# A hybrid decoder step on one core: where the norms' inverse roots are taken, and how they are spread over the partitions

## The chip, the core and the metric

One NeuronCore of a Trainium2 chip runs the whole program. The metric is the time of one execution in microseconds (us) of device time. Five engines matter: TensorE (PE, with its weight loads as PEld), VectorE (DVE), ScalarE (ACT), GpSimd (POOL), and SyncE (SP), which issues the DMAs. Each engine works through its own queue in order, and a semaphore holds an instruction until what it needs has been written.

## The reference, cut to what matters

Two layers run over 512 prompt tokens and 64 sample tokens (8 sequences of 8). Layer 0 mixes tokens by pooling, layer 1 by a gated delta rule ("GDN"). Each layer has two residual branches, and each branch has a norm before it and one after it.

```python
def rms_norm(x, gain):
    xf = x.astype(jnp.float32)
    y = xf * lax.rsqrt(jnp.mean(xf * xf, axis=-1, keepdims=True) + EPS)
    return (y * gain.astype(jnp.float32)).astype(x.dtype)

def l2norm(x):
    xf = x.astype(jnp.float32)
    return xf * lax.rsqrt(jnp.sum(xf * xf, axis=-1, keepdims=True) + EPS)
...
    for i in range(DEPTH):
        h = rms_norm(x, norm_mix_pre[i])
        ...
        x = x + rms_norm(m, norm_mix_post[i])
        h = rms_norm(x, norm_ffn_pre[i])
        x = x + rms_norm(swiglu(h, ffn_w_in[i], ffn_w_out[i]), norm_ffn_post[i])
```

`m` is the mixer's output of `h`. Inside the GDN mixer, q and k of each head go through `l2norm`, and the output of each head through `rms_norm` before it is gated.

## The kernel before, in words

Activations lie transposed: 1024 channels as 8 chunks of 128 partitions, the 576 tokens along the free dimension. The tokens are worked in two parts (`hf.i` 0 and 1), cut at a different token in different stages: 240 and 336 in the pooling mixer, 288 and 288 in the feed-forward of layer 0, 256 and 320 in layer 1. Every large matmul is done in three products of rounded halves (`mm3`: high by high, high by low, low by high), with weights split on the fly: ACT rounds them to `wh`, DVE or POOL subtracts to get `wl`.

The stages follow each other: the pooling mixer of layer 0 with its norms, the feed-forward of layer 0, then GDN (four groups of heads; `project` makes q, k, v of a group, `core` runs the delta rule, `zgate` norms and gates the output), its output product, norms, and the feed-forward of layer 1.

**Norms between the stages.** `add_sq` (ACT squares, DVE or POOL adds) leaves per partition the sum of squares of each token in `nacc`. `rstd` then does four things:

- PE multiplies each block of 128 tokens of `nacc` with a column of ones: `ps_n<-ones,nacc`, so that the sums of a block stand one per partition in one PSUM column.
- The inverse root `nrc` of these two or three columns is taken. With `on_dve` false this is ACT's `Sqrt` and DVE's `reciprocal`. With `on_dve` true it is `rsqrt` on DVE alone: `nv` (mean plus epsilon), a first guess from the bits of the number, and three Newton steps of three instructions each through `nt`.
- PE spreads `nrc` over all partitions: a matmul of the column, broadcast to 128x128, with the identity, one per block (`ps_n<-ident,nrc`).
- `post_norm` or `pre_norm` multiply the 8 chunks with gain and root on DVE.

`rstd` is called twelve times: four times in layer 0 after the mixer, four times in `finish0` after the feed-forward of layer 0, four times in layer 1 after GDN's output product. `on_dve` is true for the second part of the tokens in `post_pre` only, that is in four of the twelve. The norm at the very end (`finish1`) has its own code and stays as it is.

**Roots inside GDN.** For each of the four groups, `project` takes the inverse root of 20 columns (`rn` from `rv`) by `rsqrt` on DVE, and `gate_norm` that of 20 columns of `oss` by ACT's `Sqrt` and DVE's `reciprocal`.

**What sets the order.** No instruction is issued where it is written: the class `Plan` records all of them with what they depend on, prices each by formulas in `cost`, and orders them by a list scheduler whose priorities are shifted by numbers in the two tables of `CHOSEN`. An operation written as `EITHER` goes to DVE or POOL, whichever the planner finds better. Where PE would otherwise be idle for long, the planner puts in matmuls whose result nobody uses (`ps_w<-ones`). All recorded operations carry one line number in the profile, that of the planner's call, so groups are told apart by the names of tiles.

Of the kernel before, what the change touches and what calls it, by code (L numbers as in the profile page):

```python
# [11 lines left out]
F32 = mybir.dt.float32  # L12
F32R = mybir.dt.float32r
I32 = mybir.dt.int32
AF = mybir.ActivationFunctionType
ALU = mybir.AluOpType
# [37 lines left out]
MAGIC = float(0x5F3759DF)  # L54
# [6 lines left out]
class Plan:  # L61
# [576 lines left out]
    def cost(self, eng, method, out, ins, k):  # L638
# [26 lines left out]
        if eng == "POOL":  # L665
# [4 lines left out]
            elif method == "affine_select":  # L670
                t = 1.1 * n + 190
            else:
                bc = any(list(x.ap)[-1][0] == 0 for x in ins if self.size(x) > 1)
                t = (1.75 if bc else 2.2) * n + 180
# [1854 lines left out]
```

## Time and profile before

| | us |
|---|---|
| median of three runs | 1506.8 (1504.59 to 1508.99) |
| the profiled execution, its time | 1506.02 |
| the profiled execution, its span | 1504.3 |
| ACT busy in it | 838.9 (56%) |
| POOL busy in it | 111.1 (7%) |

The granted TensorE clock has a mean of 0.998 over the span. An engine's busy time is the union of its instructions' spans. A matmul's span overlaps the next one's, so a PE that is "busy" all the time can still be one that waits a little before each instruction; the pace of PE is better read from the starts of successive rows of the timeline. An fp32 matmul leaves two records, a transpose and an fp32r matmul one.

### The profile page before, as it was taken

To read this page: it belongs to the slowest core of one execution; us is meant where nothing else is said; L and a number is where in the kernel's file an instruction comes from. 1 tells how busy PE (TensorE), PEld (TensorE's weight loads), DVE (VectorE), ACT (ScalarE), POOL (GpSimd) and SP (SyncE) were. 2 spreads that over 40 slices of the span, in tenths; PEclk is the share of its full clock that TensorE was granted. 3 is DMA by queue.
4 is the path that set the end of the run, shared out by engine and by line. 5 is a ranking of instruction groups with operands and counts; after the bars stand their busy time and mean duration, and the time that the engine had idled before them with its cause. 6 is when DMAs were issued, how large, how long until landed. Compare 5 with 4: busy or idle time off the path is not lost.

```text
span 1504.3 us, 30115 instructions
## 1 busy us (share of the span) xinstructions
PE 1482.4 (99%) x11748; PEld 1438.1 (96%) x11748; DVE 1131.3 (75%) x2291; ACT 838.9 (56%) x1826; POOL 111.1 (7%) x240
## 2 busy tenths in 40 slices
PE   8999999999999999999999999999999999999997
PEld 8999999999999899899899899999999999999997
DVE  7995566778678697897898889557797576766855
ACT  7754443435455886675784784545574543533654
POOL 4200000000002100010121120000110000000000
PEclk9999999999999999999999999999999999999999
DMA  7642323233456433344334434757653332323262
GB/s 199 180 140 84 104 78 102 72 112 91 137 145 165 116 94 95 106 129 133 100 114 127 130 114 124 213 162 205 211 178 111 94 91 87 93 81 112 75 175 88
DMA packets 322821, 186.96 MB, mean 124 GB/s; under 512 B 13163, under 2 KB 315596, under 8 KB 322671
## 3 DMA queue, kind: packets, MB, share of 16 engines
q1 hardware_dynamic: 322679, 185.04, 42.8%
q8 instruction: 92, 1.51, 0.4%
q14 instruction: 50, 0.41, 0.1%
HBM read 154.72 MB, written 30.52 MB: 123 GB/s over the span
## 4 chain that ended last, share of the span: by engine, by line
PE 83%; DVE 6%; issue 4%; ACT 4%; DMA 2%; POOL 1%; SPq 0%; DVEq 0%; POOLq 0%; ACTq 0%
PE ps_A L804 26%; PE ps_B L804 26%; PE ps_m L804 18%; PE ps_s L804 4%; PE ps_k L804 4%; PE ps_x L804 2%; DVE wl L804 2%; PE ps_e L804 1%; DVE ac L804 1%; ACT wh L804 1%; PE ps_g L804 1%; PE ps_n L804 1%; ACT Uw L804 0%; PE ps_w L800 0%; DVE Uw L804 0%
## 5 line engine op out<-in xcount | busy, mean ns | idle before, releaser
L804 ACT ACTIVATE wh<-wraw 128x1024 fp32r<-128x1024 f32 (+4 forms) x214 | 207.9, 973 | 159.6 <-PE ps_A L804 77.0
L804 DVE TENSOR_TENSOR wl<-wraw,wh 128x1024 fp32r<-128x1024 f32 (+4 forms) x214 | 240.3, 1124 | 59.8 <-ACT wh L804 49.4
L804 PE MATMUL ps_m<-hH,wh 128*128 128x320 f32 (+1 forms) x832 | 248.5, 311 | 0.4 <-ACT u L804 0.3
L804 PE MATMUL ps_m<-hL,wh 128*128 128x320 f32 (+1 forms) x832 | 248.1, 309 | 0.0
L804 PE MATMUL ps_m<-hH,wl 128*128 128x320 f32 (+1 forms) x832 | 245.2, 308 | 0.0
L804 PEld LDWEIGHTS ps_m<-hH,wh 128*128 128x128 f32 x832 | 154.5, 189 | 4.7 <-issue 1.3
L804 PEld LDWEIGHTS ps_m<-hH,wl 128*128 128x128 f32 x832 | 154.0, 189 | 3.8 <-issue 2.1
L804 PEld LDWEIGHTS ps_m<-hL,wh 128*128 128x128 f32 x832 | 154.7, 189 | 1.6 <-issue 0.3
L804 PE MATMUL ps_B<-hL,wh 128*128 128x288 f32 (+2 forms) x420 | 123.6, 304 | 0.2 <-POOL hL L804 0.2
L804 PE MATMUL ps_B<-hH,wl 128*128 128x288 f32 (+2 forms) x420 | 123.1, 304 | 0.0
L804 PE MATMUL ps_B<-hH,wh 128*128 128x288 f32 (+2 forms) x420 | 122.3, 304 | 0.4 <-ACT hH L804 0.4
L804 PE MATMUL ps_A<-aH,wh 128*128 128x288 f32 (+2 forms) x408 | 115.4, 297 | 0.0
L804 PE MATMUL ps_A<-aH,wl 128*128 128x288 f32 (+2 forms) x408 | 115.1, 297 | 0.0
L804 PE MATMUL ps_A<-aL,wh 128*128 128x288 f32 (+2 forms) x408 | 115.1, 296 | 0.0
L804 PE MATMUL ps_A<-hH,wh 128*128 128x288 f32 (+2 forms) x396 | 108.8, 290 | 0.3 <-ACT nsq L804 0.2
L804 PE MATMUL ps_A<-hL,wh 128*128 128x288 f32 (+2 forms) x396 | 108.8, 288 | 0.0
L804 PE MATMUL ps_A<-hH,wl 128*128 128x288 f32 (+2 forms) x396 | 107.9, 289 | 0.2 <-DVE wl L804 0.2
L804 DVE SCALAR_TENSOR_TENSOR ac<-u,cwt,ac 128x600 f32<-128x600 f32 x96 | 79.8, 845 | 2.9 <-ACT ac L804 2.4
L804 PE MATMUL ps_B<-aH,wh 128*128 128x288 f32 x296 | 82.0, 296 | 0.0
L804 PE MATMUL ps_B<-aL,wh 128*128 128x288 f32 x296 | 81.7, 295 | 0.0
L804 PE MATMUL ps_B<-aH,wl 128*128 128x288 f32 x296 | 81.4, 295 | 0.3 <-DVE wl L804 0.3
L804 PEld LDWEIGHTS ps_B<-hL,wh 128*128 128x128 f32 x420 | 77.9, 188 | 0.6 <-POOL hL L804 0.5
(457 smaller groups left out, 4019.5 us busy)
## 6 DMA issues: line engine op xcount, KB each, us to landing
wraw<-in_ffn_w_in_dram SPq DMA_DIRECT2D x64, 512.0 KB
wraw<-in_gdn_w_in_dram SPq DMA_DIRECT2D x53, 512.0 KB
graw<-in_ffn_w_in_dram SPq DMA_DIRECT2D x36, 512.0 KB
wraw<-in_ffn_w_out_dram SPq DMA_DIRECT2D x26, 448.0 KB
wraw<-in_gdn_w_out_dram SPq DMA_DIRECT2D x21, 512.0 KB
wraw<-in_ffn_w_out_dram SPq DMA_DIRECT2D x32, 320.0 KB
St<-in_state_gdn_rec_dram SPq DMA_DIRECT2D x32, 256.0 KB
out_dram<-St SPq DMA_DIRECT2D x32, 256.0 KB
```

The lines of the kernel that those rows point to most:

```text
L804: calls[e](*a, **k)
```

## The change

All inverse roots in the twelve calls of `rstd`, in `project` and in `gate_norm` are now taken by one GpSimd instruction: a `tensor_tensor` with the operation power, whose second operand is a column of -0.5, broadcast. [...] The spreading over the partitions is a PE transpose of the broadcast column, block by block, in place of a matmul with the identity. Blocks that overlap are transposed whole.

```diff
+    half = cst.tile([P, 1], F32, name="half")
+    POOL.memset(half, -0.5)
...
-    def rsqrt(y, v, t):
-
-        DVE.tensor_scalar(y.bitcast(I32), v.bitcast(I32), -0.5, MAGIC, op0=mult, op1=add)
-        for _ in range(3):
-            DVE.scalar_tensor_tensor(out=t, in0=y, scalar=-0.5, in1=v, op0=mult, op1=mult)
-            DVE.tensor_tensor(t, t, y, op=mult)
-            DVE.scalar_tensor_tensor(out=y, in0=t, scalar=1.5, in1=y, op0=add, op1=mult)
+    def rsqrt(y, v):
+
+        POOL.tensor_tensor(y, v, half.to_broadcast([P, y.shape[1]]) if len(y.shape) == 2 else
+                           half.unsqueeze(2).to_broadcast([P, y.shape[1], y.shape[2]]), op=ALU.pow)
...
-        if on_dve:
-
-            v, t = (halftile(tp, w, hf, 1, (P, 4))[:, :nb] for w in ("nv", "nt"))
-            DVE.tensor_scalar(v, ps[:, :nb], 1.0 / D, EPS, op0=mult, op1=add)
-            rsqrt(rc, v, t)
-        else:
-            ACT.activation(rc, ps[:, :nb], AF.Sqrt, bias=eps_c, scale=1.0 / D)
-            DVE.reciprocal(rc, rc)
+        DVE.tensor_scalar(rc, ps[:, :nb], 1.0 / D, EPS, op0=mult, op1=add)
+        rsqrt(rc, rc)
         pr = bank("n%d" % hf.i)[:, :hf.n]
-        for i in range(nb):
-            e = min((i + 1) * P, hf.n)
-            PE.matmul(pr[:, i * P:e], rc[:, i:i + 1].to_broadcast([P, P]), ident[:, i * P - offs[i]:e - offs[i]],
-                      start=True, stop=True)
+        for i, o in enumerate(offs):
+            PE.transpose(pr[:, o:o + P], rc[:, i:i + 1].to_broadcast([P, P]), ident)
...
-                        vt_ = pp.tile([P, 2, SP1, 4], F32, name="rv", tag="rv", bufs=1)
-                        DVE.tensor_scalar(vt_[:, 0, :SPANS], ksq, EPS, None, op0=add)
-                        DVE.tensor_scalar(vt_[:, 0, SPANS], pst, EPS, None, op0=add)
-                        rsqrt(rn, vt_[:, 0], vt_[:, 1])
+                        vt_ = pp.tile([P, SP1, 4], F32, name="rv", tag="rv", bufs=1)
+                        DVE.tensor_scalar(vt_[:, :SPANS], ksq, EPS, None, op0=add)
+                        DVE.tensor_scalar(vt_[:, SPANS], pst, EPS, None, op0=add)
+                        rsqrt(rn, vt_)
...
-            ACT.activation(oss, oss, AF.Sqrt, bias=eps_c, scale=1.0 / P)
-            DVE.reciprocal(oss, oss)
+            DVE.tensor_scalar(oss, oss, 1.0 / P, EPS, op0=mult, op1=add)
+            rsqrt(oss, oss)
```

The planner gets a price for the power operation, and the two tables `CHOSEN` hold other numbers throughout, so the order of the whole program is another one. In the table only this changes in kind (first line of each):

```diff
-                t = (1.75 if bc else 2.2) * n + 180
+                t = 9.0 * n + 400 if k.get("op") == ALU.pow else (1.75 if bc else 2.2) * n + 180
...
-        "0: 5989 57171 74663 91275 358 77336 9426 78983 26827 86304 93802 31029 25971 93959 57698 79197 68511 "
```

Counted over the whole program, ACT's table loads go from 26 to 18, ACT's `Sqrt` instructions on `nrc` and `oss` from 15 to 3, and the 32 matmuls `ps_n<-ident,nrc` become 32 transposes. The matmuls that only fill idle time (`ps_w`) go from 42 to 44.

**PE, at the last of the twelve roots** (layer 1, second part of the tokens; `ps_A` is the feed-forward of the first part, which needs nothing of this root, `ps_B` that of the second part, which needs all of it). Before:

```order
L804 MATMUL ps_A<-hH,wh 128x256
L804 MATMUL ps_n_2913<-ident,nrc 128x128 x2
L804 MATMUL ps_n_2913<-ident,nrc 128x64
L804 MATMUL ps_A<-hL,wh 128x256
L804 MATMUL ps_A<-hH,wl 128x256 x2
L800 MATMUL ps_w<-ones 128x128 x2
L804 MATMUL ps_B<-hH,wh 128x320 x3
```

After, the same place:

```order
L747 MATMUL ps_A<-hL,wh 128x256
L747 MATMUL ps_A<-hH,wl 128x256 x2
L747 MATMUL ps_A<-hH,wh 128x256
L747 MATMUL ps_n_2907<-ident,nrc 128x128 x3
L747 MATMUL ps_A<-hL,wh 128x256
L747 MATMUL ps_A<-hH,wl 128x256
L747 MATMUL ps_A<-hH,wh 128x256
```

Three `ps_A` matmuls and two fillers stood between the spreading of the root and the first `ps_B`; now thirteen `ps_A` matmuls stand there, and no filler.

**DVE, at the same root.** `nv`, `nt` and `nrc` are the columns of the root, `yo<-x,prm,ps_n` multiplies the chunks with it. Before:

```order
L804 TENSOR_SCALAR nv<-ps_n_2908 128x3
L804 TENSOR_TENSOR nsq<-nsq,ps_A 128x256
L804 TENSOR_SCALAR nrc<-nv 128x3
L804 TENSOR_TENSOR aL<-nsq,aH 128x256
L804 SCALAR_TENSOR_TENSOR nt<-nrc,nv 128x3
L804 TENSOR_TENSOR wl<-wraw,wh 128x1024
L804 TENSOR_TENSOR nt<-nt,nrc 128x3
L804 TENSOR_TENSOR aL<-nsq,aH 128x256
L804 SCALAR_TENSOR_TENSOR nrc<-nt,nrc 128x3
```

After:

```order
L747 TENSOR_TENSOR wl<-wraw,wh 128x1024
L747 TENSOR_SCALAR nrc<-ps_n_2904 128x3
L747 TENSOR_TENSOR nsq<-nsq,ps_A 128x256
L747 TENSOR_TENSOR aL<-nsq,aH 128x256 x2
L747 SCALAR_TENSOR_TENSOR yo<-x_2781,prm,ps_n_2907 128x320 x4
```

Behind the rows of before come six more Newton instructions and then `yo<-x`; in the change the power stands on POOL's queue, and `yo<-x` is the fourth instruction behind the `tensor_scalar`.

**DVE, at the root of q and k in the first group of GDN** (`rv` holds the sums, `rn` the roots, `nk` and `rq` are made from them). Before:

```order
L804 TENSOR_SCALAR rv<-ps_x 128x4
L804 TENSOR_SCALAR rn<-rv 128x20
L804 SCALAR_TENSOR_TENSOR rv<-rn,rv 128x20
L804 TENSOR_TENSOR rv<-rv,rn 128x20
L804 SCALAR_TENSOR_TENSOR rn<-rv,rn 128x20
```

After:

```order
L747 TENSOR_SCALAR rv<-ksq 128x16
L747 COPY u<-cstt 128x8x3
L747 TENSOR_SCALAR rv<-ps_x 128x4
L747 TENSOR_TENSOR nk<-rn,rv 128x5x2
L747 TENSOR_SCALAR rq<-rn 128x5x2
```

Before, ten instructions on `rn` and `rv` stood between the `rv<-ps_x` row and `nk`; now `nk` follows at once and waits for POOL.

More of the change, by code (lines that the diff above doesn't have):

```diff
@@ L53 @@
 EPS = 1e-6
-MAGIC = float(0x5F3759DF)
 UW = CW - 1 + SEQ
@@ L1279, in add_sq, with rstd @@
             EITHER.tensor_tensor(acc[0], acc[0], sq, op=add)
-    def rsqrt(y, v, t):
-        DVE.tensor_scalar(y.bitcast(I32), v.bitcast(I32), -0.5, MAGIC, op0=mult, op1=add)
-        for _ in range(3):
-            DVE.scalar_tensor_tensor(out=t, in0=y, scalar=-0.5, in1=v, op0=mult, op1=mult)
-            DVE.tensor_tensor(t, t, y, op=mult)
-            DVE.scalar_tensor_tensor(out=y, in0=t, scalar=1.5, in1=y, op0=add, op1=mult)
-    def rstd(tp, acc, hf, on_dve=False):
+    def rsqrt(y, v):
+        POOL.tensor_tensor(y, v, half.to_broadcast([P, y.shape[1]]) if len(y.shape) == 2 else
+                           half.unsqueeze(2).to_broadcast([P, y.shape[1], y.shape[2]]), op=ALU.pow)
+    def rstd(tp, acc, hf):
         offs = [min(o, hf.n - P) for o in range(0, hf.n, P)]
@@ L1296, in rstd, with post_norm @@
         rc = halftile(tp, "nrc", hf, 1, (P, 4))[:, :nb]
-        if on_dve:
-            v, t = (halftile(tp, w, hf, 1, (P, 4))[:, :nb] for w in ("nv", "nt"))
-            DVE.tensor_scalar(v, ps[:, :nb], 1.0 / D, EPS, op0=mult, op1=add)
-            rsqrt(rc, v, t)
-        else:
-            ACT.activation(rc, ps[:, :nb], AF.Sqrt, bias=eps_c, scale=1.0 / D)
-            DVE.reciprocal(rc, rc)
+        DVE.tensor_scalar(rc, ps[:, :nb], 1.0 / D, EPS, op0=mult, op1=add)
+        rsqrt(rc, rc)
         pr = bank("n%d" % hf.i)[:, :hf.n]
-        for i in range(nb):
-            e = min((i + 1) * P, hf.n)
-            PE.matmul(pr[:, i * P:e], rc[:, i:i + 1].to_broadcast([P, P]), ident[:, i * P - offs[i]:e - offs[i]],
-                      start=True, stop=True)
-        return pr
-    def post_norm(tp, x, m, acc, hf, gpost, acc2, on_dve=False):
-        r = rstd(tp, acc, hf, on_dve)
+        for i, o in enumerate(offs):
+            PE.transpose(pr[:, o:o + P], rc[:, i:i + 1].to_broadcast([P, P]), ident)
+        return pr
+    def post_norm(tp, x, m, acc, hf, gpost, acc2):
+        r = rstd(tp, acc, hf)
         for c in range(NC):
@@ L1322, in post_norm, with pre_norm @@
                 add_sq(tp, acc2, xc, c, hf)
-    def pre_norm(tp, x, acc, hf, gpre, on_dve=False, keep=None):
-        r = rstd(tp, acc, hf, on_dve)
+    def pre_norm(tp, x, acc, hf, gpre, keep=None):
+        r = rstd(tp, acc, hf)
         at = slice(hf.o, hf.o + hf.n)
@@ L1335, in post_pre @@
         acc2 = []
-        post_norm(tp, x, m, acc, hf, gpost, acc2, hf.i == 1)
-        pre_norm(tp, x, acc2, hf, gpre, hf.i == 1, keep=m)
+        post_norm(tp, x, m, acc, hf, gpost, acc2)
+        pre_norm(tp, x, acc2, hf, gpre, keep=m)
     class Strassen:
@@ L1873, in finish @@
                         rn = pp.tile([P, SP1, 4], F32, name="rn", tag="rn", bufs=1)
-                        vt_ = pp.tile([P, 2, SP1, 4], F32, name="rv", tag="rv", bufs=1)
-                        DVE.tensor_scalar(vt_[:, 0, :SPANS], ksq, EPS, None, op0=add)
-                        DVE.tensor_scalar(vt_[:, 0, SPANS], pst, EPS, None, op0=add)
-                        rsqrt(rn, vt_[:, 0], vt_[:, 1])
-                        DVE.tensor_tensor(nk[:, :, hh], rn[:, :, 0:2], vt_[:, 0, :, 0:2], op=mult)
+                        vt_ = pp.tile([P, SP1, 4], F32, name="rv", tag="rv", bufs=1)
+                        DVE.tensor_scalar(vt_[:, :SPANS], ksq, EPS, None, op0=add)
+                        DVE.tensor_scalar(vt_[:, SPANS], pst, EPS, None, op0=add)
+                        rsqrt(rn, vt_)
+                        DVE.tensor_tensor(nk[:, :, hh], rn[:, :, 0:2], vt_[:, :, 0:2], op=mult)
                         DVE.tensor_scalar(rq[:, :, hh], rn[:, :, 2:4], float(P) ** -0.5, None, op0=mult)
```

879 rows, old and new, of the table CHOSEN are left out of this document.

## The prediction

> **What bounds the kernel now.** I read the page first: the busy times, then the chain that ended last, then the windows by stage.
>
> ```profile
> PE 1482.4 (99%) x11748; PEld 1438.1 (96%) x11748; DVE 1131.3 (75%) x2291; ACT 838.9 (56%) x1826; POOL 111.1 (7%) x240
> ...
> PE 83%; DVE 6%; issue 4%; ACT 4%; DMA 2%; POOL 1%; SPq 0%; DVEq 0%; POOLq 0%; ACTq 0%
> ```
>
> PE has work almost all the time, and it holds 83% of the chain. So time is won where PE gets less to do, or where PE waits; an instruction less on ACT or DVE counts only where PE waits for it. The windows by stage (length, then busy us and count by engine) tell where that can be.
>
> ```profile
> 0.00:80.00 80.00, 75.03 (x579) 70.94 (x580) 67.62 (x184) 57.99 (x136) 25.97 (x83) 1.00 0.71 196
> 420.00:480.00 60.00, 58.83 (x454) 57.15 (x453) 51.40 (x107) 31.34 (x60) 8.52 (x12) 1.00 0.60 166
> 560.00:720.00 160.00, 157.69 (x1486) 147.22 (x1485) 132.83 (x346) 99.25 (x278) 14.04 (x31) 1.00 0.42 118
> 720.00:880.00 160.00, 157.29 (x1337) 146.09 (x1336) 142.07 (x355) 110.25 (x354) 28.53 (x57) 1.00 0.43 119
> 1062.00:1120.00 58.00, 57.31 (x431) 56.05 (x430) 53.46 (x124) 36.59 (x70) 12.47 (x14) 1.00 0.59 180
> 1120.00:1440.00 320.00, 320.00 (x2403) 319.57 (x2402) 222.28 (x332) 148.21 (x225) 0.00 (x0) 1.00 0.33 96
> ```
>
> The feed-forward (1120 to 1440 us) is PE alone, without a gap, and has no root in it. The twelve roots between the stages lie in 0:80, 420:480 and 1062:1120, where DVE is busy 85%, 86% and 92%; those of GDN lie where DVE is busy 83% and 89%. PE's visible idle time there is small: 5.0, 1.2, 2.3, 2.7 and 0.7 us.
>
> **Term 1, PE's work.** 32 fp32 matmuls become 32 transposes. The tile's rows and PE's timeline at the last root give the price of both.
>
> ```profile
> L804 PE MATMUL ps_n<-ident,nrc x64: 195/275/376, 29.6 to 1111.7; 128*128 128x128 f32 x44, 128*128 128x32 f32 x8, 128*128 128x112 f32 x4, 128*128 128x80 f32 x4
> ...
> 1101.30 0.27 PE L804 MATMUL ps_n<-ident,x 128*128 128x128 f32 x1
> 1101.33 0.37 PE L804 MATMUL ps_A<-hL,wh 128*128 128x256 f32 x1
> ...
> 1111.07 0.28 PE L804 MATMUL ps_A<-hH,wh 128*128 128x256 f32 x1
> 1111.19 0.78 PE L804 MATMUL ps_n<-ident,nrc 128*128 128x128 f32 x6
> 1111.77 0.36 PE L804 MATMUL ps_A<-hL,wh 128*128 128x256 f32 x1
> 1112.22 0.60 PE L800 MATMUL ps_w<-ones 128*128 128x128 f32 x4
> 1113.18 0.71 PE L804 MATMUL ps_B<-hH,wh 128*128 128x320 f32 x3 [0.36 <-ACT hH L804]
> 1116.14 0.60 PE L804 MATMUL ps_n<-ident,x 128*128 128x128 f32 x4
> 1116.49 0.39 PE L804 MATMUL ps_B<-hH,wl 128*128 128x320 f32 x1
> ```
>
> 64 records for 32 matmuls: two each. Three of them hold PE from 1111.19 to 1111.77, 0.58 us or 0.193 each; four transposes from 1116.14 to 1116.49, 0.35 us or 0.088 each. Saved: 32 x 0.105 = **3.4 us**. It is nothing if a transpose of a broadcast column left two records; it is 5.2 us if a transpose costs only 0.03, as the one at 1101.30 does, which stands alone between two `ps_A`. I take 3.4, since most of the new ones stand in threes and twos. Nothing has to hide it: PE is full on both sides.
>
> [...]
>
> **Term 2, the Newton chain ahead of PE.** On DVE's, ACT's and PE's timelines the last root goes:
>
> ```profile
> 1107.18 0.16 DVE L804 TENSOR_SCALAR nv<-ps_n 128x3 f32<-128x3 f32 x1
> ...
> 1110.77 0.16 DVE L804 SCALAR_TENSOR_TENSOR nrc<-nt,nrc 128x3 f32<-128x3 f32 x1
> 1112.08 3.75 DVE L804 SCALAR_TENSOR_TENSOR yo<-x,prm,ps_n 128x320 f32<-128x320 f32 x8 [1.15 <-PE ps_n L804]
> ...
> 1112.66 3.68 ACT L804 ACTIVATE hH<-yo 128x320 fp32r<-128x320 f32 x8
> ```
>
> From 1107.18 to 1110.93 the root takes 3.75 us, since `wl` and `aL` work is mixed in. PE then runs out: fillers (`ps_w`) from 1112.22, and the first `ps_B` at 1113.18 on the first `hH`. That is 0.96 us of PE. In the change the root is one `tensor_scalar` (0.16) and one power, and thirteen `ps_A` matmuls (13 x 0.12 = 1.6 us, by the row at 1111.07 and the start of the next) stand behind the spreading, against the 1.0 us that `yo` and `hH` need. The wait goes: **-1.0 us**. The same chain at the second root of part 1 in layer 0 leaves fewer waits to win, since the 5.0 us of idle time in 0:80 are mostly the start; I take **-0.5 us**. The other two Newton roots stand where PE has feed-forward work: nothing. What is late next is DVE itself, at 92%: ends 0 and -2.5 us for the term.
>
> **The power's own price.** No row shows it. The nearest on POOL:
>
> ```profile
> L804 POOL MEMSET oss<- x4: 102/104/106, 483.6 to 803.5; 128x4 f32 x4
> ...
> L804 POOL TENSOR_SCALAR_AFFINE_SELECT par<-ones 32x1 f32<-32x1 f32 x4 | 2.0, 493 | 0.2
> ...
> L804 POOL TENSOR_TENSOR vt<-vt,oss x4: 1049/1268/1587, 652.1 to 896.5; 128x512 f32<-128x512 f32 x4
> ```
>
> A few columns written cost 0.1 us, one column computed 0.49, 512 columns of a broadcast product 1.27. I take 0.5 us, the row nearest in size, with ends 0.1 and 1.3. On top come held ports, as POOL's and DVE's timelines show:
>
> ```profile
> 457.07 1.68 POOL L804 TENSOR_TENSOR hL<-nh,hH 128x288 fp32r<-128x288 f32 x1 [19.77 <-ACT hH L804]
> 456.51 1.20 DVE L804 TENSOR_TENSOR wl<-wraw,wh 128x1024 fp32r<-128x1024 f32 x1
> 459.85 0.81 POOL L804 TENSOR_TENSOR hL<-nh,hH 128x288 fp32r<-128x288 f32 x1 [0.33 <-ACT hH L804]
> 71.89 1.81 POOL L804 TENSOR_SCALAR_AFFINE_SELECT eyo<-eyo 128x512 f32<-128x512 f32 x1
> 72.92 0.76 DVE L804 SCALAR_TENSOR_TENSOR nt<-nrc,nv 128x3 f32<-128x3 f32 x1
> ```
>
> POOL's `hL` took 1.68 us beside a DVE subtraction, twice the 0.81 that the next one takes at 459.85; a DVE step of 0.16 took 0.76 beside POOL. So a power can come up to a `wl` (1.2 us) late, and can hold DVE.
>
> **Term 3, the eight roots that ACT took.** At the first root of `finish0`:
>
> ```profile
> 449.45 0.24 ACT L804 ACTIVATE nrc<-ps_n,epsd 128x3 f32<-128x3 f32 x1
> 449.73 0.18 DVE L804 RECIPROCAL nrc<-nrc 128x3 f32<-128x3 f32 x1 [0.58 <-ACT nrc L804]
> 449.96 0.85 PE L804 MATMUL ps_n<-ident,nrc 128*128 128x128 f32 x6 [0.32 <-DVE nrc L804]
> ```
>
> Root and reciprocal take 0.46 us; `tensor_scalar` and power 0.16 + 0.05 + 0.5, some 0.25 more. PE waited 0.32 us here already. Two of the eight stand so that PE feels it, the first of 0:80 and this one: **+0.4 us** (ends -0.3 and +4, see the slow rival).
>
> **Term 4, GDN.**
>
> ```profile
> L804 DVE SCALAR_TENSOR_TENSOR rv<-rn,rv x12: 171/178/182, 522.4 to 876.8; 128x20 f32<-128x20 f32 x12
> L804 DVE TENSOR_SCALAR rn<-rv x4: 173/176/177, 522.2 to 874.2; 128x20 int32<-128x20 int32 x4
> ...
> L804 DVE RECIPROCAL oss<-oss x4: 266/271/276, 651.7 to 1023.2; 128x20 f32<-128x20 f32 x4
> ...
> L804 ACT ACT_TABLE_LOAD x25 | 32.1, 1283 | 1.2 <-issue 0.8
> ```
>
> Per group DVE loses ten instructions of 0.178, 1.8 us, and gets a wait of some 0.7 us in `nk`, with the subtractions of weights queued behind it; `oss` is 0.1 cheaper. That is 4 x 1.2 = 4.8 us of DVE's queue. ACT loses eight table loads of 1.283 and twelve roots of about 0.25: 13.3 us of 838.9. PE visibly idles 5.0 us in 560:880, beside DVE at 86%, so about a quarter of DVE's gain should reach it: **-1.5 us** with ACT's share (ends 0 and -5).
>
> **Sum.** -3.4 - 1.5 + 0.4 - 1.5 = **-6.0 us** against the profiled execution (span 1504.3, its time 1506.02, 0.8 under the median): **1500.0 us**. The whole order is new as well; two fillers more are 0.4 us of PE at most, and where they stand PE has nothing else to do. I give the order no sign and 3 us to both sides.
>
> **Rivals.**
> - *Only PE's work goes.* PE is busy 157.3 to 157.7 of 160 us in GDN, so ACT's and DVE's savings may be hidden throughout; then -3.4 and a little: 1503. Against it stands the filler wait at 1112.22.
> - *The power is late, and the kernel slower.* The place is the eight roots that were ACT's, four of them at a stage's first part with PE dry behind them. With the high price (1.3), a `wl` ahead on the port (1.2) and `tensor_scalar`, a root takes 2.7 us against 0.46: four times +2.2, while the Newton roots gain nothing: -3.4 + 9 = +5.6, 1512. It decides where power and hold together pass 0.46 - 0.2 + 3.4/4 = 1.1 us; over 0.3% slower needs some 2.5. POOL's 7% load speaks against it; DVE at 85% to 92%, full of `wl`, for it.
> - *The first power is special.* If POOL has to fetch code before it, the first root (29.6 us) comes late by that time L, and PE, with 5 us idle in that window already, shows L in full: 1500 + L. It eats the whole gain at L = 6. No row here shows an L. [...]
> - *DVE is the real bound of GDN.* Then all of its 4.8 us and a part of ACT's come through: -3.4 - 2.5 - 5 = 1495.
>
> **Chances.** Forecast (1497 to 1502) 0.46; only PE's work 0.25; slow power 0.11; first power 0.06; DVE bound 0.12. A measurement of this kernel tells about 0.3% from no change, that is under 1502.3 or over 1511.3 us. Faster: 0.46 + 0.12 = 0.58; same 0.25 + 0.06 = 0.31; slower 0.11. The range takes in the DVE bound with 3 us of order below, and the first power with 3 us above: 1492 to 1509.
>
> **What would show it.** Term 1: `ps_n<-ident,nrc` with 32 records in place of 64, three to 0.27 us. Term 2: no filler at the last root, and `yo<-x` some 1.5 us behind its `tensor_scalar`. The power: POOL rows `nrc<-nrc,half` near 0.5 us; over 1 us, or a first one far longer, speaks for a rival. Term 4: DVE near 1117 us busy, 18 table loads, and PE idling less than 5.0 us in 560:880. It is wrong if PE's idle time grows in 0:80 or 420:480.

## The result: 1.7% slower, and the profile after

| | before | after |
|---|---|---|
| median, us | 1506.8 (5 runs) | 1531.69 (1529.0 to 1533.96, 5 runs) |
| ratio, with its 95% interval | | 1.0166 (1.015 to 1.0182) |
| profiled execution, its time and its span, us | 1506.02, 1504.3 | 1529.0, 1527.3 |

The change costs 25 us. Where they came from is read from the starts of the first matmuls of each stage in the two timelines: `ps_e` opens GDN (with the mixer's projections), `ps_A` with a start over 1000 us opens layer 1's norms and feed-forward, `ta` the bulk of that feed-forward.

| stage, us | before | after | difference |
|---|---|---|---|
| up to the first `ps_e` | 452.0 | 448.8 | -3.2 |
| GDN, to the first `ps_A` of layer 1 | 582.7 | 610.6 | +27.9 |
| norms of layer 1, to the first `ta` | 103.7 | 101.0 | -2.7 |
| the rest | 365.9 | 366.8 | +0.9 |

So both places outside GDN got shorter, and GDN alone lost it all. The page of the changed kernel, busy times and chain:

```profile
PE 1484.5 (97%) x11720; PEld 1439.4 (94%) x11720; DVE 1123.7 (74%) x2209; ACT 831.6 (54%) x1806; POOL 147.2 (10%) x263
...
PE 55%; DVE 5%; issue 3%; POOL 2%; DMA 2%; ACT 1%; SPq 0%; DVEq 0%; POOLq 0%; ACTq 0%
```

PE's busy time did not fall by 3.4 us but grew by 2. (The shares of the chain add up to 68% here, so its 55% can't be set beside the 83% of before.) The windows of the changed kernel (length, then busy us of PE, PEld, DVE, ACT, POOL with counts; behind them the granted clock) show two things at once:

```profile
480.00:560.00 80.00, 76.41 (x570) 70.40 (x569) 58.47 (x149) 57.70 (x150) 13.56 (x25) 0.96 0.35 94
560.00:720.00 160.00, 152.63 (x1450) 143.48 (x1449) 126.22 (x311) 99.08 (x276) 24.79 (x45) 0.98 0.40 112
720.00:880.00 160.00, 153.29 (x1290) 142.32 (x1288) 132.54 (x313) 105.62 (x327) 23.33 (x46) 0.98 0.40 114
880.00:1040.00 160.00, 153.44 (x1289) 144.82 (x1288) 112.17 (x262) 87.90 (x239) 19.74 (x26) 0.99 0.49 143
```

PE idles 3.6, 7.4, 6.7 and 6.6 us there, 24.2 in all; before it was 0.3, 2.3, 2.7 and 0.6, 6.0 in all. Over the whole of GDN, which now ends at 1059.4 us, it is 27.3 us against 6.5. And the clock, 1.00 in all four windows before, is below it: PE is "busy" for longer because it runs slowly for a while. POOL's groups name the cause (mean ns behind the busy time, then the idle time ahead):

```profile
L747 POOL TENSOR_TENSOR rn<-rv,half 128x20 f32<-128x20 f32 x4 | 14.1, 3529 | 13.5 <-DVE rv L747 13.5
L747 POOL TENSOR_TENSOR oss<-oss,half 128x20 f32<-128x20 f32 x4 | 14.1, 3526 | 85.0 <-DVE oss L747 85.0
L747 POOL TENSOR_TENSOR nrc<-nrc,half 128x3 f32<-128x3 f32 x8 | 9.0, 1122 | 405.0 <-DVE nrc L747 405.0
L747 POOL TENSOR_TENSOR nrc<-nrc,half 128x2 f32<-128x2 f32 x4 | 5.0, 1251 | 70.8 <-DVE nrc L747 70.8
```

A power of 20 columns takes 3.53 us, of 2 or 3 columns a mean of 1.25 and 1.12. The planner had it at 9 ns per column and 400, that is 0.58 us for 20 columns, so its order holds little behind which the other 3 us could hide. What happens then, at the first `rn` (DVE's and PE's timelines of the changed kernel, in brackets the wait and its releaser):

```profile
517.57 0.16 DVE L747 TENSOR_SCALAR rv<-ps_x 128x4 f32<-128x4 f32 x1 [0.73 <-PE ps_x L747]
521.38 0.59 DVE L747 TENSOR_TENSOR nk<-rn,rv 128x10 f32<-128x10 f32 x1 [3.65 <-POOL rn L747]
...
521.55 0.31 PE L747 MATMUL ps_m<-hH,wh 128*128 128x320 f32 x1
525.45 1.19 PE L747 MATMUL ps_k<-qk 128*128 128x256 f32 x2 [3.59 <-DVE QD L747]
526.08 0.83 PE L747 MATMUL ps_m<-hL,wh 128*128 128x320 f32 x1
```

Nothing on DVE's queue passes the waiting `nk`: DVE stands 3.65 us there, with the steps to `QD` queued behind it, and PE stands 3.6 us for `QD`. The row at 521.55 is the last of PE's work that was planned in parallel. At the first `oss` (rows of POOL, ACT, DVE and PE) a third queue joins in:

```profile
638.85 3.53 POOL L747 TENSOR_TENSOR oss<-oss,half 128x20 f32<-128x20 f32 x1 [1.10 <-DVE oss L747]
642.34 4.28 POOL L747 TENSOR_SCALAR_AFFINE_SELECT QD<-QD 128x512 f32<-128x512 f32 x4
643.01 4.92 ACT L747 ACTIVATE QD<-QD,ngs 128x128 f32<-128x128 f32 x16 [3.19 <-POOL QD L747]
642.42 2.14 DVE L747 TENSOR_TENSOR vt<-vt,oss 128x512 f32<-128x512 f32 x2 [2.72 <-POOL oss L747]
649.50 2.04 PE L747 MATMUL ps_k<-qk 128*128 128x256 f32 x4 [6.48 <-DVE QD L747]
```

The masks `QD` stand behind the power on POOL itself, ACT waits for them, DVE waits for `oss`, and PE is dry for 6.5 us. Then comes the second price, in three windows of the changed kernel around the wait at 521.9:

```profile
516.60:523.40 6.80, 5.26 (x37) 4.79 (x35) 2.31 (x9) 6.71 (x19) 5.80 (x6) 1.00 0.44 122
523.40:530.20 6.80, 4.75 (x17) 4.26 (x17) 5.25 (x17) 0.90 (x5) 0.00 (x0) 0.50 0.29 80
530.20:533.60 3.40, 3.40 (x22) 3.19 (x22) 2.93 (x8) 3.38 (x11) 0.00 (x0) 1.00 0.00 0
```

While PE waits, its clock is halved, and stays so for 6.8 us, well into the work that follows. In the trace this happens five times in GDN: at 523.4 and 646.3 us for 6.8 us each, at 772.6, 803.3 and 895.5 us for 3.4 us each, 23.8 us at half speed. PE has work in 17.9 of them (4.75, 3.50, 3.40, 3.40 and 2.84 us), so this is worth up to 9 us.

### The profile page after: what moved, and what is told of

It reads as the page before. It is cut to its first block, busy times and chain, and to the rows that moved or that the text cites. A ratio compares the mean times of both kernels' runs of the same rounds, so it can differ in the third digit from the quotient of the medians.

```text
span 1527.3 us, 29975 instructions
## 1 busy us (share of the span) xinstructions
PE 1484.5 (97%) x11720; PEld 1439.4 (94%) x11720; DVE 1123.7 (74%) x2209; ACT 831.6 (54%) x1806; POOL 147.2 (10%) x263
## 4 chain that ended last, share of the span: by engine, by line
PE 55%; DVE 5%; issue 3%; POOL 2%; DMA 2%; ACT 1%; SPq 0%; DVEq 0%; POOLq 0%; ACTq 0%
PE ps_m L747 17%; PE ps_A L747 14%; PE ps_B L747 13%; PE ps_s L747 5%; PE ps_k L747 4%; PE ps_x L747 2%; DVE wl L747 1%; POOL oss L747 1%; POOL rn L747 1%; DVE vt L747 1%; DVE ac L747 1%; DVE yo L747 0%; DMA vt<-z_d 0%; DMA yo<-y_d 0%; DVE nacc L747 0%
## 5 line engine op out<-in xcount | busy, mean ns | idle before, releaser
L747 DVE TENSOR_TENSOR wl<-wraw,wh 128x1024 fp32r<-128x1024 f32 (+4 forms) x213 | 237.8, 1117 | 61.0 <-ACT wh L747 40.4
L747 PE MATMUL ps_m<-hH,wh 128*128 128x256 f32 (+1 forms) x832 | 249.7, 315 | 0.1
L747 PE MATMUL ps_B<-aL,wh 128*128 128x288 f32 x296 | 86.0, 296 | 0.0
L747 PE MATMUL ps_B<-aH,wh 128*128 128x288 f32 x296 | 85.1, 296 | 0.0
L747 PE MATMUL ps_B<-aH,wl 128*128 128x288 f32 x296 | 84.5, 296 | 0.2 <-DVE wl L747 0.2
L747 PEld LDWEIGHTS ps_B<-hH,wh 128*128 128x128 f32 x420 | 77.8, 188 | 0.1
```

The source lines that it names most:

```text
L747: calls[e](*a, **k)
```

## The experiments

Two theories at first. **Wide powers**: the eight powers of 20 columns are longer than their cover. **Order**: the new order is worse in itself, and the powers only happen to stand there. In the table, the ratio is to the kernel before, timed beside each run.

| run | median, us | ratio (95%) |
|---|---|---|
| wide_mult | 1498.84 | 0.9947 (0.9929 to 0.9965) |
| all_mult | 1496.62 | 0.9935 (0.9917 to 0.9952) |
| before_wide_pow | 1515.82 | 1.0058 (1.0036 to 1.008) |
| spread_only | 1506.39 | 0.9997 (0.9986 to 1.0009) |
| spread_and_narrow_pow | 1508.99 | 1.0013 (1.0001 to 1.0024) |
| wide_in_pieces | 1523.25 | 1.0111 (1.0091 to 1.0131) |
| before_plain | 1552.96 | 1.0308 (1.029 to 1.0326) |
| after_plain | 1570.1 | 1.0432 (1.0414 to 1.0451) |
| priced_plain | 1549.43 | 1.0292 (1.0277 to 1.0308) |
| norms_plain | 1559.03 | 1.035 (1.0332 to 1.0369) |
| priced | 1566.07 | 1.0394 (1.0367 to 1.0421) |
| before_searched | 1517.47 | 1.0072 (1.005 to 1.0094) |
| priced_searched | 1515.54 | 1.0058 (1.0041 to 1.0076) |
| norms_searched | 1515.41 | 1.0058 (1.0036 to 1.0081) |

### The same order without the wide powers

The planner still plans a power; only where it is issued does another operation stand, a product with a broadcast column of 0.002 (`lesser` makes it), so the order is that of the changed kernel on every engine and these roots are not computed.

```diff
                 calls, _, a, k = ops[i][:4]
+                if k.get("op") == ALU.pow and self.size(a[0]) == 20:
+                    a, k = (a[0], a[1], self.lesser(a[2])), {"op": ALU.mult}
                 calls[e](*a, **k)
```

> The changed kernel in its own order, with the eight 20-column powers of GDN (rn and oss) issued as a product with a constant on the same engine, so that these roots are not computed. Theory 1, the wide power is longer (3.53 us) than its cover: GDN, 610.6 us between the first fc matmul of the mixer and the next feed-forward in the changed kernel, comes back to 582.7 or a little less, no stretch shows a granted clock under 1.0, and the time is 1500 to 1505 us. Theory 2, the new order itself is worse in GDN: the time stays over 1520 us and the idle gaps of PE stay. Theory 3, both: in between.

It was 1498.8 us: 33 us under the changed kernel, 0.5% under before. The rows of this kernel, its busy times, POOL's group and DVE's timeline at the first `rn`, then its windows:

```profile
PE 1475.7 (99%) x11720; PEld 1432.6 (96%) x11720; DVE 1121.3 (75%) x2209; ACT 831.0 (56%) x1806; POOL 121.3 (8%) x264
...
L749 POOL TENSOR_TENSOR rn<-rv,small 128x20 f32<-128x20 f32 x4 | 0.9, 223 | 13.3 <-DVE rv L749 13.3
...
517.73 0.58 DVE L749 TENSOR_TENSOR nk<-rn,rv 128x10 f32<-128x10 f32 x1 [0.34 <-POOL rn L749]
...
480.00:560.00 80.00, 80.00 (x617) 74.48 (x617) 63.38 (x163) 60.55 (x155) 10.63 (x26) 1.00 0.38 104
560.00:720.00 160.00, 158.00 (x1494) 148.53 (x1494) 130.41 (x316) 101.14 (x289) 17.95 (x45) 1.00 0.44 122
720.00:880.00 160.00, 159.16 (x1355) 148.62 (x1354) 139.30 (x344) 115.92 (x363) 22.71 (x57) 1.00 0.43 122
880.00:1040.00 160.00, 157.83 (x1344) 149.31 (x1344) 116.67 (x253) 87.77 (x220) 7.79 (x14) 1.00 0.55 159
```

`nk` waits 0.34 us in place of 3.65, PE idles 5.0 us in the four windows in place of 24.2, and the clock is 1.00. GDN is 579.1 us long. The spans differ by 31.8 us (1527.3 and 1495.5). Of these, 23.0 us are idle time of PE (42.8 and 19.8 us over the span), and 8.8 us are longer work on the same 11720 records (1484.5 and 1475.7 us busy), about half of the 17.9 us in which PE works at half clock. So nearly three quarters of the loss are waits, and the rest is the clock. The order is not bad in itself; it is bad for a root of 3.5 us.

### The narrow powers too

> As the kernel before it, and the twelve narrow powers (2 and 3 columns) of the norms as products too, so that no root is computed. Theory 1 (narrow powers cost nearly nothing, since each is 0.7 to 0.9 us and PE has other work): within 2 us of the kernel with only the wide ones replaced. Theory 2 (the narrow ones that waited for a held port and took 1.6 to 2.0 us are felt by PE): 4 us or more under it. POOL's rows of the product say what a product of 2, 3 and 20 columns takes; I expect 0.1 to 0.3 us.

The condition on the size is left out. 1496.6 us. The medians differ by 2.2 us, but the interval overlaps that of wide_mult, and the spans are 1495.3 and 1495.5. In this order no cost of the narrow powers is clear of the noise, which speaks for theory 1.

### The wide powers in the old order

The same trick on the kernel before: its order, with the power issued at Newton's first step and in the place of the reciprocal.

```diff
+                if i in self.other:
+                    self.other[i]()
+                    continue
                 calls, _, a, k = ops[i][:4]
...
+                        plan.other[len(plan.ops)] = lambda y=rn, v=vt_[:, 0]: power(y, v)
+                        plan.other.update((len(plan.ops) + 1 + n, lambda: None) for n in range(9))
                         rsqrt(rn, vt_[:, 0], vt_[:, 1])
```

> The kernel before in its own order, with one edit: GDN's eight roots by the power (one power of 20 columns in the place of Newton's first step, the other nine left away; tensor_scalar and power in the place of the root on ACT and the reciprocal). Theory 1, the wide power by itself: slower than before by 12 to 25 us, with idle gaps of PE of 2 to 6 us behind each power and a granted clock of 0.5 behind the long ones. Theory 2, the loss came from the new order: within 5 us of before.

It lost 9.7 us (1515.82 against 1506.07), between the two theories: a power of the same 3.5 us costs here less than a third of what it costs in the changed kernel. A reason stands on DVE's timeline of this run at the first `rn`:

```profile
522.30 0.16 DVE L807 TENSOR_SCALAR rv<-ps_x 128x4 f32<-128x4 f32 x1 [1.05 <-PE ps_x L807]
523.26 0.20 DVE L807 TENSOR_SCALAR ngc<-gce 128x80 f32<-128x80 f32 x1 [0.80 <-ACT gce L807]
524.13 0.30 DVE L807 COPY nct<-u 128x3 f32<-128x3 f32 x2 [0.67 <-ACT u L807]
526.13 0.59 DVE L807 TENSOR_TENSOR nk<-rn,rv 128x10 f32<-128x10 f32 x1 [1.70 <-POOL rn L1295]
```

The order of before had been planned around ten Newton steps, so other work stands between `rv` and `nk`. PE's idle time in the four windows is 11.3 us, and its clock falls twice, for 3.4 us each. So a third theory: the loss belongs neither to the power nor to the order alone, but to **an order planned for a price six times too low**.

### The power by itself

> Not the decoder: a kernel of its own that writes zeros to the outputs and measures the power. First ten powers of 1, 2, 3, 4, 8, 12, 16, 20, 32 and 64 columns: by the rows of the changed kernel I expect 0.39 + 0.157 us per column, so 0.55, 0.70, 0.86, 1.0, 1.6, 2.3, 2.9, 3.5, 5.4 and 10.4 us; a price by instruction alone would show 0.5 to 0.9 us for all. Then 4, 20 and 64 columns with a full tile of exponents beside a product of the same size: if the cost is the power and not the broadcast, the same 1.0, 3.5 and 10.4 us, and a product of 0.2 to 0.4 us. Then three powers of 20 columns beside twelve DVE products of 1024 columns: if a power holds the port for its whole time, the two engines' times add up; if not, both run at once. Last, PE streams 220 matmuls, waits for a power of 2 to 48 columns, and streams again: it shows from which gap on the granted clock falls to 0.5, and for how long.

The first four powers ran as the formula has it, while DVE did little but write constants: 0.56, 0.71, 0.85 and 1.01 us for 1 to 4 columns. Further rows of POOL in this kernel:

```profile
34.86 3.53 POOL L45 TENSOR_TENSOR fulld<-src,full 128x20 f32<-128x20 f32 x1
38.36 0.22 POOL L46 TENSOR_TENSOR muld<-src,half 128x20 f32<-128x20 f32 x1
38.54 10.55 POOL L45 TENSOR_TENSOR fulld<-src,full 128x64 f32<-128x64 f32 x1
49.05 0.29 POOL L46 TENSOR_TENSOR muld<-src,half 128x64 f32<-128x64 f32 x1
```

The price is the power's, 0.16 us for each column, not that of the broadcast or of GpSimd's arithmetic: a product of 20 columns takes a sixteenth of it. Beside DVE's products the powers of 8, 12 and 20 columns took 2.18, 3.15 and 4.33 us, up to 0.9 longer (that of 16 columns, 3.07, only 0.2), while the twelve products of DVE took 1.21 to 1.23 us each, about what a subtraction of weights takes in the decoder (1.23 us on average in the kernel before): in this pairing it is POOL that gives way. That a port is held was the author's reading; the runs show these times, and no row shows a port. The three powers that were meant to meet the products ran behind them, undisturbed, in 3.53 us each. The part on the clock stands in the last section.

### The norms' side by itself

Two runs in the order of before: first only the transposes, then the narrow powers too.

```diff
+            plan.other[len(plan.ops)] = lambda o=offs[i], i=i: nc.tensor.transpose(
+                pr[:, o:o + P], rc[:, i:i + 1].to_broadcast([P, P]), ident)
             PE.matmul(pr[:, i * P:e], ...)
```

> The kernel before in its own order, with the 32 matmuls that spread a root issued as transposes, and nothing else. Theory 1, PE's work is what this edit saves (32 x 0.105 us): 3.4 us under before, 1502 to 1504 us. Theory 2, the matmuls were hidden behind waits for DVE at the stages' edges: no difference, within 1 us of before.

> As the one before, and the norms' twelve roots (2 and 3 columns) by tensor_scalar and power at the places of Newton's steps, or of the root on ACT and the reciprocal; GDN stays as before. Theory 1, the norms' side of the change is a gain and only GDN's powers lost it: 1 to 2 us under the kernel with the spread alone, 1500 to 1503 us, faster than before and than the changed kernel. Theory 2, the narrow powers cost as well, at the eight roots that were ACT's: 2 to 5 us over the kernel with the spread alone.

Theory 1 fell in both. The transposes save what was worked out on PE, but not in time. Busy times of the spread alone, and its window at the start:

```profile
PE 1479.5 (98%) x11716; PEld 1434.0 (95%) x11716; DVE 1129.9 (75%) x2291; ACT 838.3 (56%) x1826; POOL 112.1 (7%) x240
...
0.00:80.00 80.00, 73.56 (x567) 69.09 (x567) 67.44 (x184) 57.32 (x135) 25.66 (x82) 1.00 0.69 196
```

PE's busy time falls by 2.9 us against before, yet in the first 80 us alone its idle time grows from 5.0 to 6.4 (in the three stretches with the norms together by 2.2), and the median is that of before; the interval leaves 2.1 us less to 1.4 more. Most of the work saved comes back as waiting: the order is fixed, and what DVE and ACT hand over still sets when PE can go on. The narrow powers then add 2.6 us (the two intervals overlap a little). POOL's and PE's rows at the last root of `finish0` in that run:

```profile
470.10 1.71 POOL L1295 TENSOR_TENSOR nrc<-nrc,epsd 128x3 f32<-128x3 f32 x1 [10.63 <-DVE nrc L1313]
...
471.86 0.54 PE L1320 MATMUL ps_n<-ident,nrc 128*128 128x128 f32 x3 [1.64 <-POOL nrc L1295]
```

A DVE subtraction of weights runs from 469.87 and the power takes 1.71 us in place of 0.86; PE is dry for 1.64 us, and the clock is 0.97 in 420:480 and again in 1062:1120. The slowest of the twelve takes 3.34 us for 3 columns (at 70.88), beside two such subtractions. So of what the changed kernel wins outside GDN, the 2.7 us at layer 1 need the new order: here that stage takes 107.1 us in place of 103.7. The 3.2 us ahead of GDN do not: in the profiled execution of this run the first `ps_e` starts at 449.0 us, against 451.3 with the spread alone and 452.0 before, and the win is lost again behind it.

### The first result, or the whole length

In the changed kernel's order, each wide power cut in pieces: two for `rn`, four for `oss`.

```diff
+                    for c in range(0, 4, w):
+                        calls[e](y[:, :, c:c + w], v[:, :, c:c + w], h[:, :, c:c + w], op=ALU.pow)
```

> The changed kernel in its own order, with each wide power cut in pieces: rn in two of 10 columns (the keys' half first, which nk needs), oss in four of 5 columns, one for each head. POOL works longer (4 us for rn, 4.7 for oss, by 0.39 us + 0.157 per column), but the first result is there after 2.0 and 1.2 us. Theory 1, the wait for the first result is what is paid: PE's idle time and its half clock in GDN fall by about half, 1510 to 1518 us. Theory 2, POOL is the bound or the last piece decides: 1530 us or more.

1523.25 us, 8 us better than the changed kernel: neither number. GDN's idle time went from 27.3 to 22.5 us and its half clock from 23.8 to 13.6 us: a fifth and nearly a half. `nk` waits 2.07 us, but the next one, `rq`, waits 1.75 for the second half, and POOL's masks stand behind a longer row. The wait for the first result is part of what is paid.

### The right price in the planner

```diff
-                t = 9.0 * n + 400 if k.get("op") == ALU.pow else (1.75 if bc else 2.2) * n + 180
+                t = 157.0 * n + 390 if k.get("op") == ALU.pow else (1.75 if bc else 2.2) * n + 180
```

> The changed kernel with one number of the planner altered: a power is priced at 157 ns per column and 390 more, as the rows have it, in place of 9 and 400. The tables of seeds stay, so they were made for another price. The new order puts two to four other DVE instructions (weight subtractions of 1.2 us among them) between rv and nk, where the changed kernel had none to one. Theory 1, the powers cost what they do because the order was planned for 0.58 us: most of the 33 us between the changed kernel and the one with products in GDN comes back, 1500 to 1515 us, and few idle gaps of PE over 2 us. Theory 2, what follows a root depends on it, so nothing can cover it: 1520 to 1535 us.

1566 us, beyond both theories. Its span is 39 us over that of the changed kernel, and 29 of them lie outside GDN, where no wide power stands: the first `ps_e` comes 15 us later, and layer 1's norms take 13 us longer. So it says little about the powers. The likely reason is that the tables in `CHOSEN` (eight a kernel, not two as said above) hold only for the costs that they were made for. Without any table the same kernel is faster, as the next three show:

> The changed kernel planned without its tables of seeds, with the power at 9 ns per column: the partner of the next one, so that tables made for another price have no part in the comparison. Both theories: slower than with the tables, 1535 to 1570 us.

> As the one before, without tables, with the power at 157 ns per column and 390 more. Theory 1 (cover): 15 to 30 us faster than the one before. Theory 2 (nothing can cover it): within 5 us of it.

> The kernel before planned without its tables: what the tables are worth there, and a base for the two before this. I expect 10 to 30 us over before. Theory 1: the changed kernel without tables lies some 25 us over this one with the low price, and within 8 us of it with the right price. Theory 2: some 25 us over it with both.

Without tables the changed kernel is 17 us slower than before at the wrong price and 3.5 us faster at the right one. That fits the third theory. GDN alone takes 599.3 us in before_plain, 627.1 at the wrong price and 611.4 at the right one, so over half of what the change costs there comes back. But a fourth plain order puts a limit on it:

> The changed kernel with GDN's roots as before (Newton's steps for rn, root and reciprocal for oss), planned without tables, to be set beside before without tables (1553 us) and the changed kernel without tables at the right price (1549 us). Theory 1, the power costs some 10 us in GDN even where the planner knows its price, and the norms' side wins: 1536 to 1545 us. Theory 2, at the right price GDN's powers cost nothing: 1547 to 1552 us.

It has the power in the norms only, and lies 6 us over before_plain, against both theories; PE's clock falls in its GDN for 17 us without any power there. It even lies 9.6 us over priced_plain, which has the wide powers as well. Orders without tables scatter by that much, so this comparison suggests and does not settle. The last three got tables of their own, from the same search for each.

> The kernel before with its tables replaced by three that one search of the planner's own kind found (each seed kept if the planned end comes earlier; the same number of tables, and the same search time, for this and the next two). It is the base of the comparison: some 10 to 20 us over the kernel before, 1515 to 1527 us, since the search was shorter than what made the tables there.

> The changed kernel with the power at 157 ns per column and 390 more, and its tables replaced by three searched for that price. Theory 1, the order decides: a plan that knows the price covers most of a power, and the time is within 5 us of before_searched. Theory 2, the length decides: 9 to 20 us over before_searched, with PE's idle time in GDN 5 to 15 us longer.

> The power and the transposes in the norms only, GDN's roots as before, the right price, and three tables searched for it. Theory 1: 2 to 6 us under before_searched (the front and the second layer's norms, as in the changed kernel), and no more than 5 us under priced_searched. Theory 2: 2 to 6 us under before_searched too, but 10 us or more under priced_searched. If the narrow powers cost what the run in the order of before shows, it is not under before_searched at all.

Theory 1 held for the price: 1515.5 us against 1517.5 for before and 1515.4 for the norms alone, three intervals that overlap. All eight wide powers are there, 3.53 and 3.55 us each, and the windows of priced_searched show them covered:

```profile
480.00:560.00 80.00, 79.61 (x606) 74.04 (x606) 57.21 (x136) 62.71 (x155) 12.21 (x26) 1.00 0.39 108
560.00:720.00 160.00, 158.54 (x1469) 148.21 (x1468) 130.03 (x328) 98.48 (x278) 27.69 (x44) 1.00 0.41 115
720.00:880.00 160.00, 156.38 (x1329) 142.79 (x1329) 135.10 (x317) 104.98 (x337) 28.93 (x57) 1.00 0.40 111
880.00:1040.00 160.00, 159.28 (x1351) 151.72 (x1350) 117.67 (x272) 92.98 (x250) 23.37 (x25) 1.00 0.55 161
```

6.2 us idle, a clock of 1.00, and GDN 583.7 us long, against 583.5 in before_searched and 584.6 in norms_searched. Each is a single search, and none was made at the wrong price, so the price is tested by itself, with orders made for it, only without tables, from after_plain to priced_plain (20.7 us). No run that takes all its roots was faster than before: before_searched itself lies 11.8 us over before, so much was this search short of the one that made the tables there. Whether a longer search at the right price would bring the change under 1506 us was not tried.

## Why the prediction was wrong

It said 1500 us, between 1492 and 1509; it was 1531.7.

- **The step that failed** is "The power's own price": "I take 0.5 us, the row nearest in size, with ends 0.1 and 1.3". The rows were of other operations, and it was assumed that columns cost as little in a power as in them. For 2 and 3 columns it was inside its ends (0.70 and 0.86 us undisturbed, 1.25 and 1.12 on average), for 20 it was 3.53 us, 2.7 times the upper end. Term 4 then used it for eight roots of 20 columns with "a wait of some 0.7 us in `nk`"; the first wait was 3.65, and in all DVE stood 8.9 us at `nk`. For the other four roots it had no wait at all ("`oss` is 0.1 cheaper"); there DVE stood 10.7 us at `vt`.
- **What it did to the sum** is shown by wide_mult: with the wide roots short, the same order gives 1498.8 us, 7.2 under before, where the sum had -6.0. That the total is so close is in part luck. In the old order the transposes save no time where term 1 had -3.4, and the transposes and narrow powers together cost 2.6 us where terms 1 to 3 had -4.5. What makes up for it lies in GDN (579.1 us against 582.7) and in the new order, to which the prediction gave no sign; the runs do not part the two.
- **Term 1** was right in what it counts: 32 records, three of them from 1134.52 to 1134.82, 0.30 us where 0.27 was expected. As a term of time it holds only with a new order; "Nothing has to hide it: PE is full on both sides" fell in spread_only.
- **Term 2** came as described. The last root of the changed kernel, on POOL, PE and DVE:

```profile
1133.60 0.86 POOL L747 TENSOR_TENSOR nrc<-nrc,half 128x3 f32<-128x3 f32 x1 [9.11 <-DVE nrc L747]
1134.52 0.54 PE L747 MATMUL ps_n<-ident,nrc 128*128 128x128 f32 x3
1135.10 1.92 DVE L747 SCALAR_TENSOR_TENSOR yo<-x,prm,ps_n 128x320 f32<-128x320 f32 x4 [0.40 <-PE ps_n L747]
```

  `yo` starts 1.8 us behind its `tensor_scalar` (at 1133.30), and PE has `ps_A` throughout, no filler.
- **The rivals.** "The power is late, and the kernel slower" had the mechanism, but put it at the eight roots that were ACT's between the stages, at 1.3 us and with a DVE subtraction ahead of it. It was GDN's roots, and by length. "The first power is special" fell: the first took 1.64 us, beside a DVE subtraction, and 0.56 us for one column in pow_by_columns. The upper end of the range, 1509, counts 6 us for it, which no run shows; what the runs show are these two times. "Only PE's work goes" is not borne out by spread_only, where PE's work went and the time stayed. Whether DVE bounds GDN stays open: every run with short roots also has the new order.
- **The order.** "I give the order no sign and 3 us to both sides" was the other miss. The diff shows the planner's price of 0.58 us for 20 columns, and an order can only cover what its planner believes. before_wide_pow loses 9.7 us against before, and the changed kernel 33 against wide_mult, by the same powers. What the prediction did not have at all is the clock, which fell in or behind five waits of 2.7 to 6.5 us, over a quarter of the loss (8.8 of 31.8 us).
- **The signs that it named** told the loss only in part. The 18 table loads came. DVE was busy 1123.7 us, 7.6 less than before, where 1117 was expected. The narrow powers took over 1 us on average, which was to speak for a rival. PE idled 14.1 us in 560:880, where under 5.0 had been the sign of a gain. But the sign of being wrong, more idle time in 0:80 or 420:480, stood at 5.3 and 0.8 us against 5.0 and 1.2: it watched the norms, and the loss was in GDN.

## What to carry to other kernels

Before a new operation goes into a planned order, measure it at the size at which it will run and give the planner that price: here an order planned at a sixth of the true price lost 1.7%, while one searched for the right price came out even with the kernel before, searched the same way (1515.5 and 1517.5 us). A price taken from other operations of about the same size says nothing on how an operation grows with its columns. And work saved on the fullest engine need not be time saved: here 2.9 us less of PE's work, with the others handing over in the old order, left the time where it was. Replacing single instructions in the unchanged order tells that apart from what a new order brings.

## What the hardware showed

**In pow_by_columns the clock was halved behind every pause of 2.56 us and more, behind one of two of 1.92 us and not behind one of 1.30, and came back 3.4 us later at the earliest.** There PE streamed 220 matmuls, waited for a power, and streamed again. Its rows behind four of the waits, and windows behind the second, third and fourth; last, a row of wide_in_pieces and the window around it:

```profile
90.52 0.38 PE L68 MATMUL ps<-b,back 128*128 128x256 f32 x1 [1.30 <-DVE back L67]
148.78 0.39 PE L68 MATMUL ps<-b,back 128*128 128x256 f32 x1 [2.56 <-DVE back L67]
212.78 0.58 PE L68 MATMUL ps<-b,back 128*128 128x256 f32 x1 [4.13 <-DVE back L67]
285.10 0.58 PE L68 MATMUL ps<-b,back 128*128 128x256 f32 x1 [8.62 <-DVE back L67]
...
149.40:152.80 3.40, 3.40 (x19) 3.40 (x18) 0.00 (x0) 0.00 (x0) 0.50 0.00 0
210.90:217.70 6.80, 4.92 (x23) 4.92 (x24) 0.18 (x1) 1.61 (x1) 0.50 0.00 0
279.10:289.30 10.20, 4.20 (x19) 4.20 (x20) 0.19 (x1) 5.72 (x1) 0.50 0.00 0
...
770.97 0.67 PE L753 MATMUL ps_k<-qk 128*128 128x256 f32 x2 [2.79 <-DVE QD L753]
770.10:773.50 3.40, 2.53 (x15) 2.41 (x15) 3.26 (x12) 3.35 (x6) 0.00 (x0) 1.00 0.47 136
```

After 1.30 us it stayed up; after 1.92 us it fell in one of two cases; after 2.56 and 3.19 us it was halved for 3.4 us, after 4.13 and 6.03 for 6.8, after 8.62 for 10.2. In 149.40:152.80 PE has 19 matmuls in place of the 30 of the next 3.4 us. The length of the pause alone does not decide: in wide_in_pieces pauses of 2.79 and 2.94 us brought no fall, and in spread_and_narrow_pow pauses of 1.64 and 1.48 us did. Within pow_by_columns, and within the changed kernel, the falls start at multiples of 3.41 us from each other (180.1 and 210.9, and 772.57 and 803.29: nine of them each time). The two pauses of 1.92 us differ in where they lie in this grid: the one with a fall behind it lies between two of its points (378.25 to 380.17 us, in 378.1:381.5), and the other has one in its middle (117.41 to 119.33, with a point at 118.7). What decides in full stays open: before_searched has a fall at 1099.1 us with no pause of over 0.6 us in the 7 us before it.
